# A two-layer diffusion backbone on one core: layer 0's output projection with tokens stationary, its boundary in token order, and gate products that do not wait for their branch

## The chip, the core and the metric

The kernel runs on one core of a Trainium2 chip. The metric is the device time of one execution in microseconds (us). The kernel before takes 1455.42 us, the median of three runs (1454.31 to 1457.41). The core's engines work side by side, each through a queue of its own in the order in which the program gives it instructions: PE (TensorE, matrix products; PEld is its loading of the stationary operand), DVE (VectorE), ACT (ScalarE), POOL (GpSimd), and SP (SyncE), which here issues all DMA transfers. Engines wait for each other through semaphores.

## The reference, cut to what matters

Two layers; each reads a latent stream x (256 tokens of width 2048) and a context stream ctx (256 tokens). In layer 0 both streams go through everything; in layer 1 ctx only supplies keys and values, and the result is x.

```python
def _branch_merge(o_mla, p, lp):
    g_m = jax.nn.silu(p[..., OFF_GM:OFF_HY])
    g_h = jax.nn.silu(p[..., OFF_GH:N_IN])
    y_h = _hyena(p[..., OFF_HY:OFF_GH], lp)
    y = jnp.concatenate([rmsnorm(o_mla, lp["grp_g_mla"]) * g_m,
                         rmsnorm(y_h, lp["grp_g_hy"]) * g_h], axis=-1)
    return rmsnorm(y @ lp["w_out"], lp["post_g"])

def _layer(x, ctx, c, c_ctx, lp, cos, sin, update_ctx):
    ...
    hx = rmsnorm(x, lp["pre_g"]) * (1.0 + sc_x) + sh_x
    px = hx @ lp["w_in"]
    ...
    o_x = o_x.swapaxes(0, 1).reshape(B, L, MLA_W)
    x_new = x + g_x * _branch_merge(o_x, px, lp)
```

`p` is one input projection. It holds queries and keys of an attention branch (A), three inputs of a long-convolution branch (B), and a gate for each branch. `shift`, `scale` and gate `g_x` come from a vector of the stream through `ada_w` (the modulation).

## The kernel before

**Layout.** Activations stand with features on the 128 partitions and tokens in the free dimension ("transposed"). A layer's 16 tiles of features (KT = 16) hold 512 columns: 256 of ctx (stream 0), then 256 of x (stream 1). Each product of two f32 operands is made as three: both operands are split in a high and a low part (`split`, line 428: a CAST on ACT for the high part, a subtraction on DVE for the low), and `mm3` (line 448) multiplies high by high, high by low, low by high. A matmul is named out<-moving,stationary. Products that are not split (sums over partitions with a ones matrix, tables of the Fourier transform) leave two records each in the trace.

**Items.** The big products go by weight items of 1024 columns (0.5 MB): `w_items` (line 840) cuts a projection into items; `loader` loads them, `prepper` splits them, `products` (line 988) runs their matmuls into `acc` tiles of PSUM, strictly in the order of a list of 362 items. After the last item of a group, an evacuation ("evac") brings the sums to SBUF. An item with a `need` is not begun before the named steps have been recorded. Items 90 to 125 are layer 0's branch inputs, 126 to 157 its gates, 158 to 221 its output projection (first x, then ctx), 222 on layer 1: queries, keys and values, branch inputs, 294 to 325 gates, 326 to 361 output projection.

**Order.** All other work (attention heads, convolution, norms, the boundary) stands in jobs, Python generators that yield one instruction at a time. `Net.run` (line 364) records the next instruction of that job which could start first by a table of costs, and of those within 0.05 us the one of best rank. Products have the worst rank (10): they fill what jobs leave. The recorded order is what the engines get; nothing is reordered on the chip. A pool of 78 tiles of 128x512 (`slots`, "s" in names) limits who may begin.

**Gates.** `layer_items` (line 1523) gives the last item of each gate group a need: `on{l}_{i}` (branch A's rows i are normalised) or `hn{l}_{i}` (branch B's). Its evac (`gate_evac`, line 1387) takes SiLU of the sums on ACT and multiplies the branch's row with it on DVE. The normalisation (`branch_norm`, line 1212) uses `rstd_bc` (line 484): a sum of squares over partitions by a ones matmul, a power of -1/2 on POOL, and two transposes that spread the result over partitions.

**Output projection and boundary of layer 0.** For each stream and each 256 output features, the weights are stationary and the stream's 256 tokens move: 128x256 matmuls. `z_evac` (line 1410) copies the sums and adds up their squares. Behind a stream's last item `boundary` (line 1421) starts: `rstd_bc` over the features; z times gate times norm, plus the old residual, which `hx_job` (line 825) had written to DRAM as `xt_d` and which is fetched back; a second `rstd_bc`; `modulate` (line 810) makes layer 1's input `hx1`. For stream 1 the new residual is transposed back to token rows and written to `xres_d`, which the end of layer 1 reads. x's boundary runs beside ctx's projection, ctx's boundary beside layer 1's first items. Layer 1's projection already runs with tokens stationary (`rows=True`).

Of the kernel before, what the change touches and what calls it, by code (L numbers as in the profile page):

```python
# [9 lines left out]
F32 = mybir.dt.float32  # L10
# [159 lines left out]
class Net:  # L170
# [330 lines left out]
    def setup(self):  # L501
# [10 lines left out]
        nc.vector.memset(self.ones, 1.0)  # L512
        self.mhalf = c.tile([P, 1], F32, name="mhalf")
# [269 lines left out]
    def first_norm(self):  # L783
# [24 lines left out]
        self.xt_d = self.scratch("xt_d", [KT, P, T])  # L808
# [16 lines left out]
    def hx_job(self, t0, t1):  # L825
        hx = self.st[0].setdefault("hx", {})

        def one(kt):
            hx[kt] = yield from self.new_split(T)
            yield from self.modulate(0, kt, self.xt[kt], self.bc0, hx[kt], ((0, slice(0, L)), (1, slice(L, T))))  # L830
        yield from self.each(one(kt) for kt in range(t0, t1))
        self.done.add(f"hx0_{t0}")
        if t1 == KT:
            self.slots.put(self.bc0)
            for kt in range(KT):
                yield self.dma(self.xt_d[kt], self.xt[kt])
                self.slots.put(self.xt[kt])
# [374 lines left out]
    def branch_norm(self, l, sq, src, base, gain, nq, flag):  # L1212
# [5 lines left out]
        for h0 in range(0, 8, 2):  # L1218
# [168 lines left out]
    def gate_evac(self, l, tile0, nq):  # L1387
        st = self.st[l]

        def evac(m, ps):  # L1390
            g = (yield from self.sget())[0]
            yield self.act(g[:, 0:nq], ps[:, 0:nq], AF.Silu)
            y = st["y"][tile0 + m][:, 0:nq]
            yield self.tt(y, y, g[:, 0:nq], ALU.mult)
            self.slots.put(g)
            if (tile0 + m) % 8 == 7:
                self.done.add(f"y{l}_{tile0 // 8}")
        return evac

# [9 lines left out]

    def z_evac(self, s, g):  # L1410
        st = self.st[0]

        def evac(m, ps):
            z = st.setdefault("z", {})
            if m == 0:
                z[s, g] = (yield from self.sget())[0]
            yield self.either(z[s, g][:, m * L:(m + 1) * L], ps[:, 0:L])
            yield from self.sumsq(st.setdefault("z_sq", {}).setdefault(s, [None]), ps[:, 0:L], L)
        return evac

    def boundary(self, s):
        st = self.st[0]
        bc = yield from self.rstd_bc([(st["z_sq"][s], L)], D)
        sq = [None]
        xn = {}
        xr = {}
        r = slice(s * L, (s + 1) * L)
        pc = self.par[0]["pcol"]

        def fetch(g):  # L1430
            if g < 8:
                xr[g] = (yield from self.sget())[0]
                for m in range(2):
                    yield self.dma(xr[g][:, m * L:(m + 1) * L], self.xt_d[2 * g + m][:, r])
        yield from fetch(0)
        yield from fetch(1)
        for g in range(8):
            z = st["z"][s, g]
            yield from self.on(xr[g], bc)
            for m in range(2):  # L1440
                h = z[:, m * L:(m + 1) * L]
                yield self.stt(h, h, pc[:, 2 * g + m, s:s + 1], bc[:, 0:L])
            yield self.tt(z, z, xr[g], ALU.add)
            self.slots.put(xr.pop(g))
            yield from fetch(g + 2)
            yield from self.sumsq(sq, z, T)
            xn[g] = z
        (h,) = yield from self.sget()
        yield self.tt(h[:, 0:L], sq[0][:, 0:L], sq[0][:, L:T], ALU.add)
        self.slots.put(bc, sq[0])  # L1450
        bc = yield from self.rstd_bc([([h], L)], D)
        hx = self.st[1].setdefault("hx", {})
        p = self.par[1]
        for kt in range(KT):
            src = xn[kt // 2][:, (kt % 2) * L:(kt % 2 + 1) * L]
            hx[s, kt] = yield from self.new_split(L)
            yield from self.modulate(1, kt, src, bc, hx[s, kt], ((s, slice(0, L)),))
            if kt % 4 == 3:
                self.done.add(f"hx1_{s}_{kt // 4}")
            if kt % 2:  # L1460
                if s == 0:
                    self.slots.put(xn[kt // 2])
        self.slots.put(bc)
        if s == 0:
            return
        self.xres_d = self.scratch("xres_d", [2, 4, P, 512])
        for g in range(4):
            for tt in range(2):
                (ps,) = yield from self.pget()
                for q in range(4):  # L1470
                    kt = 4 * g + q
                    yield self.tr(ps[:, q * P:(q + 1) * P],
                            xn[kt // 2][:, (kt % 2) * L + tt * P:(kt % 2) * L + (tt + 1) * P], self.ident)
                (t,) = yield from self.sget()
                yield self.act(t, ps)
                self.mis.put(ps)
                yield from self.on(t)
                yield self.dma(self.xres_d[tt, g], t)
                self.slots.put(t)
            self.slots.put(xn[2 * g], xn[2 * g + 1])  # L1480


    def out_evac(self, g):
        st = self.st[1]

        def evac(m, ps):
# [8 lines left out]
            yield self.tt(st["zo"][m][g], ps, self.gate[g], ALU.mult)  # L1495
        return evac

    def load_gate(self):
        self.gate = []
        p = self.par[1]["pcol"]  # L1500
        for j in range(4):
# [297 lines left out]
```

## Time and profile before

| | us |
|---|---|
| median of the runs | 1455.42 |
| profiled execution, its time | 1454.14 |
| profiled execution, first to last instruction (span) | 1452.4 |
| PE busy | 1410.2 |
| DVE busy | 1230.0 |
| ACT busy | 690.6 |
| POOL busy | 17.3 |

Busy time is the union of an engine's instructions; a matmul's record is longer than its share of PE, since matmuls are pipelined, and so a step on PE is read from full stretches, as length over count. In views of groups, a row gives engine, operation, out<-in, shape and count, then busy us, mean ns of one, and the idle time before with what ended it. In a timeline a row gives start, length, and in brackets the idle time before it.

### The profile page before, as it was taken

The page shows a single profiled execution, that of the slowest core. Times are in us where ns is not written, and L with a number is a line of the kernel's source. Part 1 is how long each engine was busy: PE and PEld are TensorE (multiplying, and loading weights), DVE is VectorE, ACT ScalarE, POOL GpSimd, SP SyncE. Part 2 cuts the span into 40 slices and gives each one's busy share as a digit, 9 for nine tenths or more (in the row PEclk, how much of TensorE's full clock was granted, in tenths as well). Part 3 has the DMA queues.
Part 4 walks back from the last instruction along what each step waited for, and adds up shares of the span by engine and source line. Part 5 has one row for each costly group of instructions (what it writes and reads, how often), then busy time and mean ns, then how long its engine had stood idle before and what let it go on. Part 6 is the DMA issues. An engine that isn't in the chain of part 4 may idle for free.

```text
span 1452.4 us, 24747 instructions
## 1 busy us (share of the span) xinstructions
PE 1410.2 (97%) x9184; PEld 1239.1 (85%) x9184; DVE 1230.0 (85%) x2283; ACT 690.6 (48%) x1325; POOL 17.3 (1%) x20
## 2 busy tenths in 40 slices
PE   7899899999999999999999999999999999899997
PEld 5676678788888888888889999998999998899886
DVE  4669899999999999998899979769989998885554
ACT  4421345455445452444325436564556666455542
POOL 0000000000000000000000000000000000000000
PEclk9999999999999999999999999999999999999999
DMA  9999864456555677446759854488859544676631
GB/s 315 335 333 358 292 245 142 163 177 236 192 192 178 206 254 259 147 146 219 266 211 369 283 204 138 168 301 311 304 189 345 199 151 164 214 241 223 236 122 58
DMA packets 146281, 329.87 MB, mean 227 GB/s; under 512 B 16325, under 2 KB 38892, under 8 KB 146160
## 3 DMA queue, kind: packets, MB, share of 16 engines
q1 hardware_dynamic: 146160, 328.29, 64.9%
q8 instruction: 72, 1.18, 0.3%
q14 instruction: 49, 0.40, 0.1%
HBM read 303.04 MB, written 25.18 MB: 226 GB/s over the span
## 4 chain that ended last, share of the span: by engine, by line
PE 78%; DMA 12%; DVE 6%; issue 2%; SPq 1%; ACT 1%; POOL 0%; DVEq 0%; POOLq 0%; ACTq 0%
PE acc L233 61%; PE mis L233 14%; DVE s L251 4%; PE mis L236 2%; DMA raw<-in_p_ada_first 2%; DMA s<-in_p_win 2%; DMA raw<-in_p_win 1%; DMA s<-in_p_ada_first 1%; SPq L310 1%; DMA ring<-in_p_ada_slow 1%; DMA s<-in_filt_w 1%; DMA s<-in_p_uk 1%; DVE junk L281 1%; DMA s<-in_ctx 1%; DVE raw L251 1%
## 5 line engine op out<-in xcount | busy, mean ns | idle before, releaser
L233 PE MATMUL acc<-s,hi 128*128 128x256 f32 (+1 forms) x2336 | 559.6, 330 | 6.8 <-DVE s L251 4.0
L233 PE MATMUL acc<-s,s 128*128 128x256 f32 (+1 forms) x2928 | 496.6, 324 | 0.4 <-ACT s L244 0.2
L233 PEld LDWEIGHTS acc<-s,s 128*128 128x128 f32 x2928 | 430.3, 191 | 45.4 <-issue 2.3
L233 PEld LDWEIGHTS acc<-s,hi 128*128 128x128 f32 x2336 | 393.0, 191 | 45.9 <-DVE s L251 5.3
L233 PE MATMUL acc<-s,raw 128*128 128x256 f32 (+1 forms) x1120 | 368.9, 329 | 1.6 <-DVE raw L251 1.6
L251 DVE TENSOR_TENSOR s<-s,s 128x512 fp32r<-128x512 f32 (+6 forms) x545 | 322.1, 619 | 26.7 <-ACT s L244 15.2
L281 DVE SCALAR_TENSOR_TENSOR junk<-ring,ring 128x1024 bf16<-128x1024 f32 x240 | 292.1, 1217 | 13.7 <-DMA ring<-in_p_ada_slow 11.2
L233 PE MATMUL mis<-s,s 128*128 128x256 f32 (+1 forms) x1232 | 239.0, 336 | 2.4 <-ACT s L244 1.0
L233 PEld LDWEIGHTS acc<-s,raw 128*128 128x128 f32 x1120 | 213.9, 191 | 20.6 <-DVE raw L251 2.6
L233 PEld LDWEIGHTS mis<-s,s 128*128 128x128 f32 x1232 | 190.5, 189 | 31.8 <-DVE s L251 4.2
L244 ACT CAST s<-s 128x512 fp32r<-128x512 f32 (+2 forms) x294 | 162.8, 586 | 88.9 <-DVE s L251 27.4
L244 ACT CAST hi<-raw 128x1024 fp32r<-128x1024 f32 (+1 forms) x97 | 94.1, 970 | 139.6 <-PE acc L233 97.4
L251 DVE TENSOR_TENSOR raw<-raw,hi 128x1024 fp32r<-128x1024 f32 x85 | 103.6, 1220 | 36.2 <-ACT hi L244 35.9
L244 ACT CAST hi<-s 128x512 fp32r<-128x512 f32 x134 | 79.3, 618 | 108.7 <-PE acc L233 90.5
L251 DVE TENSOR_TENSOR raw<-s,hi 128x512 fp32r<-128x512 f32 x134 | 90.4, 684 | 40.9 <-ACT hi L244 35.4
L244 ACT COPY s<-mis 128x512 f32<-128x512 f32 (+3 forms) x99 | 47.4, 481 | 127.8 <-PE mis L233 88.8
L244 ACT CAST s<-mis 128x512 fp32r<-128x512 f32 (+1 forms) x100 | 56.5, 569 | 78.2 <-PE mis L236 45.8
L251 DVE TENSOR_TENSOR s<-raw,s 128x512 fp32r<-128x512 f32 x132 | 87.2, 683 | 3.4 <-ACT s L244 3.4
L251 DVE TENSOR_TENSOR s<-mis,s 128x512 fp32r<-128x512 f32 (+2 forms) x128 | 84.6, 666 | 5.9 <-ACT s L244 2.7
L244 ACT CAST s<-raw 128x512 fp32r<-128x512 f32 x132 | 77.7, 618 | 15.4 <-DMA raw<-in_p_win 12.8
L236 PE MATMUL mis<-ident,s 128*128 128x128 f32 x365 | 67.6, 292 | 5.8 <-ACT s L244 2.7
L236 PEld LDWEIGHTS mis<-ident,s 128*128 128x128 f32 x365 | 49.1, 155 | 19.7 <-ACT s L244 3.8
(85 smaller groups left out, 824.2 us busy)
## 6 DMA issues: line engine op xcount, KB each, us to landing
ring<-in_p_ada_slow SPq DMA_DIRECT2D x136, 512.0 KB, 4.1
raw<-in_p_win SPq DMA_DIRECT2D x105, 512.0 KB, 5.1
s<-in_p_win SPq DMA_DIRECT2D x166, 256.0 KB, 5.5
s<-in_p_wout SPq DMA_DIRECT2D x100, 256.0 KB, 5.7
raw<-in_p_wout SPq DMA_DIRECT2D x46, 512.0 KB, 3.6
s<-in_p_ada_first SPq DMA_DIRECT2D x62, 256.0 KB, 5.9
raw<-in_p_ada_first SPq DMA_DIRECT2D x25, 512.0 KB, 6.6
ring<-crow_d SPq DMA_DIRECT2D x14, 512.0 KB, 5.9
```

The source lines that it names most:

```text
L233: lambda: self.nc.tensor.matmul(out, lhsT, rhs, start=start, stop=stop), 0.3)
L236: return Op("pe", 0.11, [out], [in_], lambda: self.nc.tensor.transpose(out, in_, ident), 0.3)
L244: self.nc.scalar.copy(out, in_)
L251: return Op("dve", fixed + n * rate, [out], ins, lambda: getattr(self.nc.vector, name)(out=out, **kw))
L281: lambda: self.nc.vector.scalar_tensor_tensor(out=junk, in0=a, scalar=1.0, in1=b, op0=ALU.mult, op1=ALU.mult, accum_out=acc))
L310: return Op("sp", n / 360e3, [dst], [src], lambda: self.nc.sync.dma_start(dst, src))
```

## The change

Layer 0's output projection takes the split activations as stationary operand, 128 tokens at a time, and moves 512 weight columns (`rows=True`, weights laid out as layer 1's). Its result stands in token rows. `z_evac` takes the squares with ACT's accumulation and multiplies with the modulation gate, which `gate_rows` writes to DRAM as a row and `gate_load` reads back broadcast over partitions. `boundary` works on token rows: x and ctx are read again from the inputs (`residual`), both norms are numbers per partition (`rstd_rows`, no PE work), the residual is written as it stands, and the normalised rows are transposed by PE, four 128x128 at a time, into layer 1's layout. `xt_d` is gone, and a tile of x becomes free as soon as it is modulated. `load_gate` of layer 1 uses the same broadcast. Gate items have no need any more; the product of gate and branch is recorded by whichever comes last (`gated`). An item of the projection needs two tiles of activations where it needed four.

```diff
@@ hx_job
             yield from self.modulate(0, kt, self.xt[kt], self.bc0, hx[kt], ((0, slice(0, L)), (1, slice(L, T))))
+            self.slots.put(self.xt[kt])
...
-            for kt in range(KT):
-                yield self.dma(self.xt_d[kt], self.xt[kt])
-                self.slots.put(self.xt[kt])
@@ branch_norm
                 self.done.add(f"{flag}{l}_{h}")
+                yield from self.gated(l, base + h, nq)
@@ gate_evac
             yield self.act(g[:, 0:nq], ps[:, 0:nq], AF.Silu)
-            y = st["y"][tile0 + m][:, 0:nq]
-            yield self.tt(y, y, g[:, 0:nq], ALU.mult)
...
+            st.setdefault("g", {})[tile0 + m] = g
+            yield from self.gated(l, tile0 + m, nq)
...
+    def gated(self, l, i, nq):
+        st = self.st[l]
+        flag = ("on", "hn")[i // 8]
+        if i not in st.get("g", {}) or f"{flag}{l}_{i % 8}" not in self.done:
+            return
+        g = st["g"].pop(i)
+        y = st["y"][i][:, 0:nq]
+        yield self.tt(y, y, g[:, 0:nq], ALU.mult)
...
+    def gate_load(self, l, s):
+        g = yield from self.sget(4)
+        for j in range(4):
+            yield self.dma(g[j], self.gate_d[l, s][:, j * 512:(j + 1) * 512].to_broadcast([P, 512]))
+        self.gate[l, s] = g
@@ z_evac
-            yield self.either(z[s, g][:, m * L:(m + 1) * L], ps[:, 0:L])
-            yield from self.sumsq(st.setdefault("z_sq", {}).setdefault(s, [None]), ps[:, 0:L], L)
+            yield from self.until((f"gate0_{s}",))
+            (junk,) = yield from self.sget()
+            yield self.act(junk, ps, AF.Square, accum_out=self.zss[:, s, m, g:g + 1])
+            self.slots.put(junk)
+            (z[s, m, g],) = yield from self.sget()
+            yield self.tt(z[s, m, g], ps, self.gate[0, s][g], ALU.mult)
...
+    def residual(self, s, m, h):
+        z = self.st[0]["z"]
+        xr = yield from self.sget(4)
+        src = self.a["x" if s else "ctx"]
+        for g in range(4):
+            yield self.dma(xr[g], src[0, m * P:(m + 1) * P, g * 512:(g + 1) * 512])
+        rs = yield from self.rstd_rows(self.zss[:, s, m])
+        for g in range(4):
+            x = z[s, m, g]
+            yield from self.on(xr[g])
+            yield self.stt(x, x, rs, xr[g], ALU.mult, ALU.add)
+            yield self.act(xr[g], x, AF.Square, accum_out=self.xss[:, s, m, g:g + 1])
+        self.slots.put(*xr)
+        rs = yield from self.rstd_rows(self.xss[:, s, m])
+        for g in range(4):
+            x = z[s, m, g]
+            (h[m, g],) = yield from self.sget()
+            yield self.act(h[m, g], x, AF.Copy, scale=rs)
+            if s == 1:
+                yield self.dma(self.xres_d[m, g], x)
@@ boundary
-        bc = yield from self.rstd_bc([(st["z_sq"][s], L)], D)
...
+        yield from self.each(self.residual(s, m, h) for m in range(2))
...
+        for kp in range(KT // 2):
+            (ps,) = yield from self.pget()
+            for i in range(2):
+                kt = 2 * kp + i
+                for m in range(2):
+                    yield self.tr(ps[:, i * L + m * P:i * L + (m + 1) * P],
+                                  h[m, kt // 4][:, (kt % 4) * P:(kt % 4 + 1) * P], self.ident)
...
+                yield self.act(t[:, r], ps[:, r], AF.Identity, bias=p["mcol"][:, 0, kt, s:s + 1],
+                               scale=p["acol"][:, kt, s:s + 1])
+            self.mis.put(ps)
+            v = yield from self.to_split(t, T)
@@ load_gate
-        for j in range(4):
-            self.gate.append((yield from self.spread(p[:, 4 * j:4 * j + 4, 1], T)))
+        yield from self.gate_rows(1)
+        yield from self.gate_load(1, 1)
@@ layer_items
-                it = win(g0 + g, self.gate_evac(l, 8 * half + 2 * g, nq))
-                it[-1].need = (f"{flag}{l}_{2 * g + 1}",)
-                gates.append(it)
+                gates.append(win(g0 + g, self.gate_evac(l, 8 * half + 2 * g, nq)))
@@ build
-            for g in range(8):
+            for g in range(4):
...
-                items += self.w_items(a["p_wout0"][g], 256, lambda kt, r=r: self.st[0]["ys"][kt][:, r],
-                                      self.z_evac(s, g), need)
+                items += self.w_items(a["p_wout0"][g], 512, lambda kt, r=r: self.st[0]["ys"][kt][:, r],
+                                      self.z_evac(s, g), need, rows=True)
```

The change moves instructions on every engine, since the recorded order is a result of the whole. Three places on PE matter here. First, the beginning of layer 0's output projection (item 158), before:

```order
L233 MATMUL acc_99_7540<-s_897_7151,hi_62_7390 128x256
L233 MATMUL acc_99_7540<-s_898_7152,hi_62_7390 128x256
L233 MATMUL acc_99_7540<-s_897_7151,raw_154_7391 128x256
L233 MATMUL acc_100_7541<-s_897_7151,hi_62_7390 128x256
L233 MATMUL acc_100_7541<-s_898_7152,hi_62_7390 128x256
L233 MATMUL acc_100_7541<-s_897_7151,raw_154_7391 128x256
```

and of the change (here the weights' parts stand in slots s, 928 and 930; the activations' parts are 906 and 907):

```order
L233 MATMUL acc_99_7541<-s_928_7431,s_906_7320 128x512
L233 MATMUL acc_99_7541<-s_930_7433,s_906_7320 128x512
L233 MATMUL acc_99_7541<-s_928_7431,s_907_7321 128x512
L233 MATMUL acc_100_7542<-s_928_7431,s_906_7320 128x512
L233 MATMUL acc_100_7542<-s_930_7433,s_906_7320 128x512
L233 MATMUL acc_100_7542<-s_928_7431,s_907_7321 128x512
```

Six matmuls of 256 columns for one tile of inputs and 256 output features have become six of 512 columns for one tile of inputs and 512 output features. Second, PE around the norm of branch A in layer 1 (`on1`: the ones matmul and the two transposes <-ident,rs), before; mis_326 is the last head's output, and acc rows are gate products, the first of item 297:

```order
L233 MATMUL mis_326_14350<-s_1777_14323,s_1709_13880 128x256
L233 MATMUL mis_326_14350<-s_1778_14324,s_1709_13880 128x256
L233 MATMUL mis_326_14350<-s_1777_14323,s_1710_13881 128x256
L233 MATMUL mis_327_14377<-ones,s_1560_12837 128x1 x2
L236 MATMUL mis_328_14391<-ident,rs 128x128 x2
L233 MATMUL acc_165_13974<-s_1200_9881,hi_141_13803 128x256 x2
L233 MATMUL acc_165_13974<-s_1200_9881,raw_297_13804 128x256
```

and of the change, the rows up to the same two transposes; 324, 325, 327 and 328 are matmuls of the convolution job, acc_149 is a product of item 296:

```order
L233 MATMUL mis_325_13428<-s_1772_13356,s_1467_11283 128x512
L233 MATMUL mis_325_13428<-s_1773_13357,s_1467_11283 128x512
L233 MATMUL mis_325_13428<-s_1772_13356,s_1468_11284 128x512
L233 MATMUL mis_326_13434<-ones,s_1546_11873 128x1 x2
L233 MATMUL acc_149_13200<-s_1168_8915,hi_138_13065 128x256
L233 MATMUL mis_327_13451<-s_1784_13413,s_1467_11283 128x512
L233 MATMUL mis_327_13451<-s_1785_13414,s_1467_11283 128x512
L233 MATMUL mis_327_13451<-s_1784_13413,s_1468_11284 128x512
L233 MATMUL mis_328_13452<-s_1784_13413,s_1467_11283 128x512
L233 MATMUL mis_328_13452<-s_1785_13414,s_1467_11283 128x512
L233 MATMUL mis_328_13452<-s_1784_13413,s_1468_11284 128x512
L236 MATMUL mis_329_13459<-ident,rs 128x128 x2
```

Before, nothing stands between the last head, the ones matmul and the transposes. Now nineteen instructions stand between the last head's last matmul and the ones matmul (four transposes, nine products, six matmuls of 128x512), and seven behind it. Third, PE at the boundary of the context stream, in layer 1's first items; before, a piece of the first norm (ones) beside transposes of x's residual:

```order
L233 MATMUL acc_132_10130<-s_1162_9547,hi_97_10020 128x256 x2
L233 MATMUL acc_132_10130<-s_1162_9547,raw_225_10021 128x256
L233 MATMUL mis_234_10169<-ones,s_1119_8985 128x1
L236 MATMUL mis_235_10186<-ident,s_1085_8670 128x128 x2
L236 MATMUL mis_235_10186<-ident,s_1106_8827 128x128 x2
L233 MATMUL mis_234_10169<-ones,s_1119_8985 128x1
```

and of the change, the first transposes of normalised context rows (s_1239 and s_1251) inside item 230:

```order
L233 MATMUL acc_120_9628<-s_1145_8765,hi_103_9557 128x256
L233 MATMUL acc_120_9628<-s_1144_8764,raw_228_9558 128x256
L236 MATMUL mis_232_9664<-ident,s_1239_9525 128x128
L236 MATMUL mis_232_9664<-ident,s_1251_9604 128x128
L236 MATMUL mis_232_9664<-ident,s_1239_9525 128x128
L236 MATMUL mis_232_9664<-ident,s_1251_9604 128x128
```

PE's part in the boundary moves from the sums at its two norms to groups of four transposes, the first in the ninth item after the stream's last projection item.

More of the change, by code (lines that the diff above doesn't have):

```diff
@@ L512, in setup @@
         nc.vector.memset(self.ones, 1.0)
+        self.zss = c.tile([P, 2, 2, 4], F32, name="zss")
+        self.xss = c.tile([P, 2, 2, 4], F32, name="xss")
+        self.gate = {}
         self.mhalf = c.tile([P, 1], F32, name="mhalf")
@@ new lines, in evac, with rstd_rows @@
+            yield from self.until((f"gate0_{s}",))
[4 more added lines that the diff above has]
+            yield self.tt(z[s, m, g], ps, self.gate[0, s][g], ALU.mult)
+        return evac
+    def rstd_rows(self, sums):
+        ms = self.small.tile([P, 4], F32, tag="mf", name="mf")
+        rs = self.small.tile([P, 4], F32, tag="rf", name="rf")
+        yield self.vsum(ms[:, 0:1], sums)
+        yield from self.rstd_cols(rs[:, 0:1], ms[:, 0:1], D)
+        return rs[:, 0:1]
@@ L1452, in boundary @@
+    def boundary(self, s):
+        if s == 1:
+            self.xres_d = self.scratch("xres_d", [2, 4, P, 512])
+        self.slots.put(*self.gate[0, s])
+        h = {}
+        yield from self.each(self.residual(s, m, h) for m in range(2))
         hx = self.st[1].setdefault("hx", {})
         p = self.par[1]
[L1454 to L1480, printed above, removed]
+        for kp in range(KT // 2):
+            (ps,) = yield from self.pget()
+            for i in range(2):
[3 more added lines that the diff above has]
+                                  h[m, kt // 4][:, (kt % 4) * P:(kt % 4 + 1) * P], self.ident)
+            if kp % 2:
+                self.slots.put(h[0, kp // 2], h[1, kp // 2])
+            (t,) = yield from self.sget()
+            for i in range(2):
+                kt = 2 * kp + i
+                r = slice(i * L, (i + 1) * L)
+                yield self.act(t[:, r], ps[:, r], AF.Identity, bias=p["mcol"][:, 0, kt, s:s + 1],
+                               scale=p["acol"][:, kt, s:s + 1])
+            self.mis.put(ps)
+            v = yield from self.to_split(t, T)
+            self.slots.put(t)
+            for i in range(2):
+                c = v[:, i * L:(i + 1) * L]
+                hx[s, 2 * kp + i] = Split(c.hi, c.lo, [v.tiles[i]])
+            if kp % 2:
+                self.done.add(f"hx1_{s}_{kp // 2}")
@@ L1508, in load_gate @@
             self.xres.append(r)
-        yield from self.on(*self.gate)
+        yield from self.on(*self.gate[1, 1])
     def finish(self, m):
@@ L1549, in layer_items @@
         gates = []
-        for half, (g0, flag) in enumerate(((G_GM, "on"), (G_GH, "hn"))):
+        for half, g0 in enumerate((G_GM, G_GH)):
             for g in range(4):
-                it = win(g0 + g, self.gate_evac(l, 8 * half + 2 * g, nq))
-                it[-1].need = (f"{flag}{l}_{2 * g + 1}",)
-                gates.append(it)
+                gates.append(win(g0 + g, self.gate_evac(l, 8 * half + 2 * g, nq)))
         return q, kvs, mids, gates
@@ L1770, in lay_out @@
     o["p_wkr"] = w[:, :, OFF_KR:OFF_GM].reshape(2, 4, 4, P, 64).transpose(0, 1, 3, 2, 4).reshape(2, 4, P, 256)
-    o["p_wout0"] = tiles(i["w_out"][0:1])[0]
-    o["p_wout1"] = i["w_out"][1].reshape(8, 2, P, 4, 512).transpose(3, 0, 2, 1, 4).reshape(4, 8, P, 1024)
+    for l in range(2):
+        o[f"p_wout{l}"] = i["w_out"][l].reshape(8, 2, P, 4, 512).transpose(3, 0, 2, 1, 4).reshape(4, 8, P, 1024)
     uq = i["w_uq"].reshape(2, 4, P, HEADS, HEAD_Q)
```

66 lines of the change are left out of this document (26 added, 40 removed).

## The prediction

> **What bounds the kernel now.** I read the page first: span, busy shares, the clock strip and the chain of waits.
>
> ```profile
> span 1452.4 us, 24747 instructions
> PE 1410.2 (97%) x9184; PEld 1239.1 (85%) x9184; DVE 1230.0 (85%) x2283; ACT 690.6 (48%) x1325; POOL 17.3 (1%) x20
> PE 78%; DMA 12%; DVE 6%; issue 2%; SPq 1%; ACT 1%; POOL 0%; DVEq 0%; POOLq 0%; ACTq 0%
> ```
>
> The reader should see that TensorE is busy for 97% of the span and carries 78% of the chain that ended last. DVE at 85% is near, so DVE must be followed too. A mean hides stages, so next come the stretches of the span (columns: window, length, busy us and instructions of PE, weight loads, DVE, ACT, POOL; granted clock; DMA share; GB/s).
>
> ```profile
> 0.00:100.00 100.00, 86.64 (x771) 63.16 (x771) 57.24 (x123) 39.12 (x90) 1.32 (x6) 0.98 0.93 322
> ...
> 100.00:160.00 60.00, 53.86 (x552) 40.34 (x552) 52.35 (x103) 16.63 (x34) 0.00 (x0) 1.00 0.97 358
> 400.00:500.00 100.00, 100.00 (x510) 84.31 (x509) 95.16 (x182) 48.41 (x90) 0.00 (x0) 1.00 0.58 197
> 600.00:700.00 100.00, 99.90 (x462) 81.91 (x461) 89.50 (x156) 41.16 (x66) 1.47 (x1) 1.00 0.66 220
> 700.00:800.00 100.00, 100.00 (x568) 88.29 (x567) 94.58 (x155) 39.44 (x73) 0.00 (x0) 1.00 0.75 272
> 800.00:900.00 100.00, 100.00 (x837) 100.00 (x836) 87.31 (x159) 48.63 (x98) 0.70 (x1) 1.00 0.60 204
> 900.00:1000.00 100.00, 97.48 (x799) 96.57 (x797) 76.69 (x141) 54.86 (x106) 3.76 (x3) 0.98 0.70 240
> 1200.00:1300.00 100.00, 93.78 (x683) 88.19 (x683) 82.72 (x167) 57.47 (x118) 2.15 (x2) 0.98 0.61 202
> ```
>
> Up to about 160 us DMA is 93 to 97% busy and PE waits; from then on PE is full, except near 985 us (layer boundary) and 1260 us (layer 1's gates), which are also the stretches with a clock under 1.00. So the time is PE's own work plus a few waits, and I cost the change in these two currencies.
>
> **Part 1: the projection.** Layer 0's projection (768 to 957 us) has 64 weight items of 24 matmuls of 128x256, 1536 in all. The change makes 64 items of 12 matmuls of 128x512, 768. Layer 1's projection already has the new form (tokens stationary, 512 weight columns moving), so both prices stand in one answer, PE alone: first the old form, then the new.
>
> ```profile
> 770.00:860.00 90.00, 90.00 (x753) 1.00 0.89 319
> 1357.00:1440.00 83.00, 83.00 (x368) 1.00 0.38 128
> ```
>
> PE is full in both, so time over count is the step: 90.00/753 = 0.1195 us and 83.00/368 = 0.2255 us. Old: 1536 x 0.1195 = 183.6 us. New: 768 x 0.2255 = 173.2 us. **Term: -10.4 us.** Nothing lies beside it, since PE was full there; weight bytes, splitting of weights and item order stay the same. The new rate asks 0.5 MB per 12 x 0.2255 = 2.7 us, 194 GB/s, and the old stage ran at 319 GB/s with PE full.
>
> The Trainium skill, "TensorE: Matmul & The Clock Gate", section "Back-to-back issue gap", gives an isolated warm gap of N/2.4 + 2.5 ns, 109 and 216 ns for these two widths. By it halving the count saves only 768 x 2.5 ns = 1.9 us, an estimate from that page. The two rows disagree: 2 x 0.1195 - 0.2255 = 0.0135 us per pair, and the measurement decides.
>
> **Part 2: PE's small work.** Four blocks of "sum of squares over partitions, then spread to a row" leave the boundary: 16 records of the ones matmul and 8 transposes. Also gone are the 32 transposes that turn the residual back to rows and the 16 that spread layer 1's gate. Added are 64 transposes that turn the normalised rows to columns, and 3 for the gates.
>
> ```profile
> 1263.02 0.58 PE L233 MATMUL mis<-ones,s 128*128 128x1 f32 x4 [2.57 <-DVE s L251]
> 957.63 0.60 PE L236 MATMUL mis<-ident,s 128*128 128x128 f32 x4
> L236 PE MATMUL mis<-ident,s 128*128 128x128 f32 x357 | 65.8, 292 | 5.4 <-ACT s L244 2.4 <-DMA s<-in_x 1.1 <-DMA s<-in_ctx 0.8
> L233 PE MATMUL mis<-ones,s 128*128 128x1 f32 x68 | 8.7, 238 | 4.4 <-DVE s L251 4.4
> ```
>
> In a row of four, the last ends 0.29 us (0.24 for ones) after its start, so a step is (0.60 - 0.29)/3 = 0.10 us and (0.58 - 0.24)/3 = 0.11 us. Net: 16 x 0.11 out, 67 - 56 = 11 x 0.10 in. **Term: -0.7 us.**
>
> **Part 3: the gates' wait.** Before, a gate product whose evacuation needs the branch's normalised rows may not start until those are recorded, and every PE job behind it stands still. Layer 1's branch A, on PE:
>
> ```profile
> 1259.59 0.86 PE L233 MATMUL mis<-s,s 128*128 128x256 f32 x5 [0.47 <-DVE s L251]
> 1265.36 0.69 PE L236 MATMUL mis<-ident,rs 128*128 128x128 f32 x2 [1.76 <-POOL rs L303]
> 1264.80:1268.20 3.40, 2.84 (x14) 0.51 0.90 280
> 1268.20:1272.00 3.80, 3.80 (x33) 0.99 0.90 299
> ```
>
> PE idles 0.47, 2.57 (the ones row quoted above) and 1.76 us, and then runs at a clock of 0.51 for 3.40 us: 14 starts where 3.40/0.1195 = 28 would fit. In the new order, between head 7's last matmul and the ones matmul stand 4 transposes, 9 matmuls of 256 and 6 of 512: 4 x 0.10 + 9 x 0.1195 + 6 x 0.2255 = 2.8 us, over the 2.57. Between ones and spread stand one of 256 and six of 512, 1.5 us of the 1.76. The 0.47 stays. Term: -2.57 - 1.5 = **-4.1 us**, and without the idle the slow clock window should go: 14 steps lost x 0.1195 = 1.7, of which some 0.2 us is the rest of the wait: **-1.5 us**. In layer 0 (gates from 564 to 768 us) PE is full, as 600:700 and 700:800 show, so nothing is gained there.
>
> What is late next: the gate products that were held back no longer cover branch B. In the new order its sum stands at item 308 of 362, and the output projection, which needs it, begins at 326: 18 items x 24 x 0.1195 = 52 us. Before it was 305, so the cover shrinks by 9 us and remains.
>
> **Part 4: the boundary.** Its waits before, on PE:
>
> ```profile
> 908.72 0.43 PE L236 MATMUL mis<-ident,rs 128*128 128x128 f32 x2 [0.58 <-POOL rs L303]
> 960.18 0.38 PE L233 MATMUL mis<-ones,s 128*128 128x1 f32 x2 [0.28 <-DVE s L251]
> 986.65 0.58 PE L233 MATMUL mis<-ones,s 128*128 128x1 f32 x4 [1.51 <-DVE s L251]
> 988.40:991.80 3.40, 3.40 (x19) 0.50 0.58 191
> ```
>
> The first two belong to the boundary and go; the third is layer 1's query norm, followed by a half-clock window that starts 19 matmuls where 28 fit, 1.1 us. The new boundary puts its first transposes nine items after the stream's last product, and these wait for loads of x, two row norms and the scaling. Prices, by form:
>
> ```profile
> L281 DVE SCALAR_TENSOR_TENSOR junk<-ring,ring 128x1024 bf16<-128x1024 f32 x240 | 292.1, 1217 | 13.7 <-DMA ring<-in_p_ada_slow 11.2 <-DMA s<-in_p_win 1.1
> L251 DVE TENSOR_TENSOR s<-s,s 128x512 fp32r<-128x512 f32 x216 | 141.3, 683 | 9.7 <-ACT s L244 9.6
> L251 DVE TENSOR_TENSOR raw<-raw,hi 128x1024 fp32r<-128x1024 f32 x85 | 103.6, 1220 | 36.2 <-ACT hi L244 35.9
> L251 DVE SCALAR_TENSOR_TENSOR s<-s,rf,s 128x512 f32<-128x512 f32 x8 | 5.5, 748 | 1.3 <-POOL rf L303 1.3
> L244 ACT CAST s<-raw 128x512 fp32r<-128x512 f32 x132 | 77.7, 618 | 15.4 <-DMA raw<-in_p_win 12.8 <-DMA raw<-in_p_wout 2.5
> L246 ACT ACTIVATION_READ_ACCUMULATOR s<-acc 128x1 f32 x8 | 1.5, 193 | 0.0
> ```
>
> For the latent stream the cover is the second stream's projection: the order has 25 us of ACT and 21 us of DVE work beside 31 us of PE before the first transposes. No wait. For the context stream, from its last product to its last transposes, PE has 426 rows: 390 x 0.1195 and 36 small ones, 50.5 us. DVE has 81, among them 27 subtractions of 512 at 0.683, 11 dots at 1.217, 8 residual steps at 0.748 and 4 subtractions of 1024 at 1.22, with the small ones 54 us. ACT has 80, about 47 us (618 ns a cast, 0.19 more for each accumulated square). So DVE is over PE by some 4 us here. Bounds: from -3.5 us (all the waits above and the slow window go, none comes) to +5 us (DVE's 4 us and a second slow window against the 0.9 us of the first two waits). I take 0: DVE's excess pays back the 0.9, the 1.5 and the 1.1 us.
>
> The transfers (KB each, median us from issue to landing):
>
> ```profile
> xt_d<-s SPq DMA_DIRECT2D x16, 256.0 KB, 3.7
> ...
> s<-xt_d SPq DMA_DIRECT2D x32, 128.0 KB, 5.4
> ...
> s<-in_x SPq DMA_DIRECT2D x8, 256.0 KB, 6.3
> ```
>
> The 16 spills go; 16 loads of 256 KB of x and ctx, 6.3 us each, replace the 32 loads of 128 KB. The gates' 12 broadcast loads of 256 KB stand in SP's queue over ten items ahead of their first reader, so products hide them too.
>
> **Part 5: the start.** Slots come free tile by tile, so loads are issued in another order. Up to the last first-layer modulation weight, SP issues 49.8 MB where it issued 50.9. At 358 GB/s (window 100:160) that is 2.9 us at most, either way if the new order is the worse. PE's waits there have many causes; I take 0.
>
> **Sum.** -10.4 - 0.7 - 4.1 - 1.5 = -16.7 us on the profiled execution's 1454.14 gives 1437.4. The median of the runs, 1455.42, lies 1.3 us above that execution: **1438.7 us**.
>
> **Rivals.**
> - **The waits come back elsewhere.** PE's order changes throughout; parts 3 and 4 rest on an order recorded before the chip's delays. If the 5.6 us of part 3 return, at the boundary or among the heads of layer 1, 1444; with the boundary at +5 as well, 1449. For it: DVE at 95% in 400:500. Against: PE is at 100.00 in that very stretch. Chance 0.28.
> - **It does better:** the boundary's -3.5 and the start's -2.9: 1432. Chance 0.12.
> - **It doesn't do what it says: the projection's step gains nothing.** If a 512-wide matmul with layer 0's operands took as long as two of 256, 0.239 us, part 1 would be 0: 1449. The two PE rows speak against it. Chance 0.03. The Trainium skill's gap formula of part 1 lies near this rival, 1.9 us under it.
> - **Slower: the boundary's transposes hold PE.** They stand in PE's queue between products, so each group of four that finds its rows unready stops all of layer 1 behind it. There are 16 groups, one per 3 to 3.5 us of PE. Slower than before needs 16.7 us of waiting, over 1.0 us for each of the 16; at 1.5 us each the time is 1438.7 + 24 = 1463. For it: DVE's 54 us against 50.5 in the second stream. Against: that is 4 us in all, and the first stream has 10 us to spare. Chance 0.05.
>
> - **The transposes slow the clock.** If each of the 16 groups cost a window like that at 988.40, 1.1 us, the time is 1438.7 + 17.6 = 1456, no change. Chance 0.02, because the old residual transposes speak against it:
>
> ```profile
> 945.00:962.00 17.00, 16.72 (x144) 1.00 0.79 273
> ...
> 945.00:962.00 17.00, 4.83 (x32) 1.00 0.79 273
> ```
>
> The first row is all of PE, the second its transposes (line 236) alone: 32 of the 144, in groups of four among products, and the clock stayed at 1.00. This rival is a rule of the Trainium skill, "TensorE: Matmul & The Clock Gate", section "Part 4: PE-mode transpose": a transpose does not count as PE-busy in the way a matmul does, and the fast clock does not engage for it.
>
> **How the numbers follow.** The forecast has 0.50. A change of 0.2%, 2.9 us, is about what a measurement of this kernel can tell from none. Faster by more than that: 0.50 + 0.12 + 0.03 + nearly all of 0.28, 0.92; within it 0.03, the slow clock and the worst of the returned waits; slower 0.05. The range, 1431 to 1449, takes in the better case and the returned waits and leaves out the slow rival.
>
> **What would show it.** In the profile after: 768 projection matmuls of 128x512 in some 175 us with PE full; no idle before layer 1's first ones and spread beyond 1 us, and no half-clock window there; the transposes of the second boundary with waits of about 4 us in total. The forecast is wrong if the projection's step is not near 0.2255 us, if PE idles over 5 us at the boundary, or if the first 200 us move by more than 3.

## The result, and the profile after

The changed kernel takes 1434.47 us (median of four runs, 1434.05 to 1436.47) against 1455.07 us before (1454.31 to 1457.41, four runs): a ratio of 0.9855, 95% interval 0.9836 to 0.9874, or 20.6 us. The forecast was 1438.7 us in a range of 1431 to 1449. The profiled execution took 1436.47 us, 17.7 us less than that of before; the sum had said 16.7. The other 2.9 us lie between the profiled executions and the medians: before, the profiled one was 0.9 us under the median, after, 2.0 us over it (it is the longest of the four).

The page after, same lines as before:

```profile
span 1434.7 us, 23168 instructions
PE 1400.1 (98%) x8411; PEld 1200.3 (84%) x8411; DVE 1196.2 (83%) x2186; ACT 691.6 (48%) x1329; POOL 18.1 (1%) x24
PE 82%; DMA 7%; DVE 6%; issue 2%; ACT 1%; SPq 1%; DVEq 0%; POOLq 0%; POOL 0%; ACTq 0%
```

PE has 773 instructions and 10 us of busy time less and a larger share of the chain. So the bound is the same engine with less work. The stretches (window, length, then busy us and count for PE, weight loads, DVE, ACT, POOL; clock; DMA share; GB/s):

```profile
900.00:1000.00 100.00, 99.43 (x655) 91.10 (x654) 87.73 (x151) 70.28 (x144) 4.41 (x5) 1.00 0.93 344
...
1100.00:1200.00 100.00, 96.41 (x688) 89.80 (x687) 80.59 (x163) 58.58 (x117) 0.00 (x0) 0.98 0.39 130
1200.00:1300.00 100.00, 100.00 (x780) 96.90 (x780) 86.17 (x176) 59.45 (x124) 1.77 (x2) 1.00 0.60 199
```

The reader is to see that PE's two holes of before (900 to 1000 and 1200 to 1300) are closed but for 0.6 us, and that a new one has opened at 1100 to 1200, with the clock at 0.98. Before, that stretch was full:

```profile
1100.00:1200.00 100.00, 100.00 (x752) 95.80 (x751) 96.45 (x194) 63.05 (x125) 0.00 (x0) 1.00 0.60 210
```

PE alone in the changed kernel, inside layer 0's projection and inside layer 1's:

```profile
780.00:860.00 80.00, 80.00 (x355) 1.00 0.84 300
...
1340.00:1420.00 80.00, 80.00 (x354) 1.00 0.37 125
```

80.00/355 = 0.2254 us a matmul of 512 columns, the same in both layers. Following items through the recorded order, the first matmul of layer 1 (item 222) comes 178.8 us after the first of the projection (item 158), where it came 189.0 us after it: -10.2 us. The projection itself begins at 768.2 us in both profiled executions, so between these two nothing was gained or lost ahead of it. At layer 1's branch A norm, in the timeline of PE:

```profile
1247.16 0.50 PE L233 MATMUL mis<-ones,s 128*128 128x1 f32 x4
...
1249.11 0.38 PE L236 MATMUL mis<-ident,rs 128*128 128x128 f32 x2
```

No bracket stands behind these rows (one would from 0.15 us on): PE did not idle before them, where it had idled 2.57 and 1.76 us. The new hole, on PE and then on ACT:

```profile
1115.98 0.28 PE L233 MATMUL acc<-s,raw 128*128 128x256 f32 x1
1117.24 0.50 PE L233 MATMUL acc<-s,hi 128*128 128x256 f32 x2 [0.98 <-ACT hi L244]
1118.60 0.48 PE L233 MATMUL acc<-s,raw 128*128 128x256 f32 x1 [0.86 <-DVE raw L251]
```

```profile
1113.23 1.28 ACT L246 ACT_TABLE_LOAD   x1 [7.95 <-DVE sm L251]
1114.52 0.69 ACT L246 ACTIVATE s<-mis,sm 128x512 f32<-128x512 f32 x1
...
1116.16 1.03 ACT L244 CAST hi<-raw 128x1024 fp32r<-128x1024 f32 x1
```

ACT stood 7.95 us at an exponential of the first attention head, which waited for its maximum from DVE. The CAST that splits the next weight item stood behind it in ACT's queue, and PE waited for that CAST. Two waits of under 1 us were followed by one window of 3.4 us at half clock. A second profile of the same kernel (after_b, below) has the same two waits without the window; first this execution, then that one, PE alone:

```profile
1118.70:1122.10 3.40, 3.40 (x17) 0.51 0.01 2
```

```profile
1119.50:1122.90 3.40, 3.40 (x29) 1.00 0.01 2
```

### The profile page after: what moved, and what is told of

Its sections match the earlier page's. It is cut to its first block, busy times and chain, and to the rows that moved or that the text cites. A ratio compares the mean times of both kernels' runs of the same rounds, so it can differ in the third digit from the quotient of the medians.

```text
span 1434.7 us, 23168 instructions
## 1 busy us (share of the span) xinstructions
PE 1400.1 (98%) x8411; PEld 1200.3 (84%) x8411; DVE 1196.2 (83%) x2186; ACT 691.6 (48%) x1329; POOL 18.1 (1%) x24
## 4 chain that ended last, share of the span: by engine, by line
PE 82%; DMA 7%; DVE 6%; issue 2%; ACT 1%; SPq 1%; DVEq 0%; POOLq 0%; POOL 0%; ACTq 0%
PE acc L233 64%; PE mis L233 15%; DVE s L251 4%; PE mis L236 3%; DMA s<-in_p_uv 2%; DVE junk L281 1%; DMA raw<-in_p_ada_first 1%; SPq L310 1%; DVE raw L251 1%; DMA s<-in_ctx 1%; DMA s<-in_p_win 1%; DMA s<-in_filt_w 1%; ACT s L246 1%; DMA ring<-in_p_ada_slow 1%; DMA s<-in_p_ada_first 1%
## 5 line engine op out<-in xcount | busy, mean ns | idle before, releaser
L233 PE MATMUL acc<-s,hi 128*128 128x512 f32 (+1 forms) x1824 | 479.1, 350 | 5.4 <-DVE s L251 3.8
L233 PE MATMUL acc<-s,s 128*128 128x512 f32 (+1 forms) x2556 | 476.0, 340 | 0.2 <-ACT s L244 0.2
L233 PEld LDWEIGHTS acc<-s,hi 128*128 128x128 f32 x1824 | 318.4, 192 | 49.3 <-DVE s L251 4.6
L233 PE MATMUL acc<-s,raw 128*128 128x512 f32 (+1 forms) x864 | 303.4, 351 | 2.9 <-DVE raw L251 2.9
L244 ACT CAST s<-s 128x512 fp32r<-128x512 f32 (+3 forms) x338 | 187.0, 590 | 61.9 <-DVE s L251 25.1
L233 PEld LDWEIGHTS acc<-s,raw 128*128 128x128 f32 x864 | 165.5, 192 | 24.1 <-DVE raw L251 3.6
L233 PE MATMUL acc<-hi,s 128*128 128x512 f32 x344 | 111.6, 390 | 0.0
L244 ACT CAST s<-mis 128x512 fp32r<-128x512 f32 x100 | 55.9, 569 | 62.4 <-PE mis L236 32.5
L236 PE MATMUL mis<-ident,s 128*128 128x128 f32 (+1 forms) x397 | 71.1, 290 | 4.6 <-DVE s L268 1.5
L233 PEld LDWEIGHTS acc<-hi,s 128*128 128x128 f32 x344 | 64.5, 188 | 13.2
```

The lines of the kernel that those rows point to most:

```text
L233: lambda: self.nc.tensor.matmul(out, lhsT, rhs, start=start, stop=stop), 0.3)
L236: return Op("pe", 0.11, [out], [in_], lambda: self.nc.tensor.transpose(out, in_, ident), 0.3)
L244: self.nc.scalar.copy(out, in_)
```

## The experiments

Each run has the kernel before on the same chip beside it, so I compare ratios to it; 0.1% is 1.5 us. "Changed" is the changed kernel.

### The step of a matmul

halves cuts the projection's matmuls in two, with the same tile standing still:

```diff
@@ w_items
-                        if rows:
+                        if rows and cols:
+                            t = x[:, m * P:(m + 1) * P]
+                            for n3, (u, v) in enumerate(((t.hi, w.hi), (t.hi, w.lo), (t.lo, w.hi))):
+                                step = wid if (first and n3 == 0) or (last and n3 == 2) else cols
+                                for c in range(0, wid, step):
+                                    yield self.mm(ps[:, c:c + step], u, v[:, j * wid + c:j * wid + c + step],
+                                                  first and n3 == 0, last and n3 == 2)
+                        elif rows:
...
@@ build
-                                      self.z_evac(s, g), need, rows=True)
+                                      self.z_evac(s, g), need, rows=True, cols=256)
```

> The changed kernel with layer 0's projection matmuls cut in two of 256 columns, same stationary tile, all but the first and the last of each sum (32 of 512, 1472 of 256 in place of 768 of 512). Theory (a step of 0.1195 us for 256 and 0.2255 for 512 whatever stands still): +736 x 0.0135 = +9.9 us, 1444.4. Rival (the gain came from which operand stands still, or a second matmul on the same stationary tile is cheaper): less than half of it, under 1439.5.

Measured: 1443.77 us, ratio 0.9915 [0.9903, 0.9928], against 0.9855 for the changed kernel: 0.6% or 8.7 us more. From item 158 to item 222 it took 188.3 us, 9.5 us more than the changed kernel, and within 0.7 us of the old 189.0. So the gain comes from the number of matmuls, not from which operand stands still.

### The gates with and without their need

need_both restores the needs in the changed kernel; its edit stands below. gates_only puts the gates' part of the change (`gated`, no needs) alone into the kernel before.

```diff
@@ layer_items
-        for half, g0 in enumerate((G_GM, G_GH)):
+        for half, (g0, flag) in enumerate(((G_GM, "on"), (G_GH, "hn"))):
             for g in range(4):
-                gates.append(win(g0 + g, self.gate_evac(l, 8 * half + 2 * g, nq)))
+                it = win(g0 + g, self.gate_evac(l, 8 * half + 2 * g, nq))
+                it[-1].need = (f"{flag}{l}_{2 * g + 1}",)
+                gates.append(it)
```

> The changed kernel with the gate items' needs put back in both layers (projection, boundary and spill stay changed). Theory of the prediction (part 3: the waits around layer 1's branch A norm went because gate products no longer wait): they come back, +5.6 us on the changed kernel's 1434.5, so 1440, with idle of about 2.6 and 1.8 us before the ones matmul and the spread near item 296 and a half-clock window behind. Rival (those waits went because the whole order moved: in this kernel's order nine matmuls of 128x512 still stand between the last head and the ones matmul, and three behind it): at most 1 to 2 us of wait, no slow window, 1435 to 1437.

> The kernel before with the gates' part of the change alone. Theory of the prediction: -5.6 us on 1455.1, so 1449.5, no idle at the norm of branch A in layer 1, where its order now has products between the ones matmul and the spread. Rival (the gates' part is worth nothing by itself, what it removes comes back as other waits): 1455.

gates_only: 1451.59 us, ratio 0.9960 [0.9947, 0.9974], by the ratio 5.8 us less than before (3.8 to 7.7), where 5.6 was expected. Its recorded order is that of before up to item 297. In its timeline the two rows at the norm have no idle ahead of them, but behind them a transpose of the convolution waits 2.26 us, where before had no wait:

```profile
1265.97 0.50 PE L233 MATMUL mis<-ones,s 128*128 128x1 f32 x4
...
1268.32 0.38 PE L236 MATMUL mis<-ident,rs 128*128 128x128 f32 x2
...
1289.15 0.55 PE L236 MATMUL mis<-ident,s 128*128 128x128 f32 x3 [2.26 <-DVE s L268]
```

From item 288 to item 326 the same PE work took 177.1 us, against 181.3 before: 4.2 us less. So part of the gain came back as another wait, as the rival had it, and the 5.8 agrees with 5.6 only within its interval.

need_both: 1446.88 us, ratio 0.9942 [0.9928, 0.9955]. That is 0.9% or 13 us over the changed kernel, more than either side expected, and not where part 3 had looked. Layer 1's waits did not come back in size; around its norm PE waited 0.23 us:

```profile
1258.66 0.50 PE L233 MATMUL mis<-ones,s 128*128 128x1 f32 x4
1259.02 0.94 PE L233 MATMUL mis<-s,s 128*128 128x512 f32 x3
1260.19 0.43 PE L236 MATMUL mis<-ident,rs 128*128 128x128 f32 x2 [0.23 <-POOL rs L303]
```

The loss stands in layer 0, at branch B's norm: from item 142 to item 158 PE took 109.0 us, where the changed kernel took 92.7; from item 158 to item 361 it was 2.9 us faster. First the timeline (acc rows are products, mis<-s,s and mis<-ident,s the convolution), then the window in which the clock is 0.50:

```profile
688.65 0.39 PE L233 MATMUL acc<-s,raw 128*128 128x512 f32 x1
688.88 0.84 PE L233 MATMUL mis<-s,s 128*128 128x512 f32 x3
...
695.24 0.98 PE L236 MATMUL mis<-ident,s 128*128 128x128 f32 x7 [0.62 <-ACT s L244]
696.05 0.50 PE L233 MATMUL mis<-ones,s 128*128 128x1 f32 x4
703.84 1.01 PE L233 MATMUL mis<-ones,s 128*128 128x1 f32 x4 [7.28 <-DVE s L251]
707.11 1.11 PE L236 MATMUL mis<-ident,rs 128*128 128x128 f32 x4 [2.26 <-POOL rs L303]
707.88 6.46 PE L233 MATMUL acc<-s,s 128*128 128x512 f32 x17
```

```profile
699.20:712.80 13.60, 6.70 (x20) 0.50 0.88 296
```

PE idles 7.28 and 2.26 us, and four windows pass at half clock. In this order items 143 and 144 are recorded whole; then come the convolution's last 20 instructions on PE and the norm's 8 with no product between them, since item 145, the next, needs the norm's rows. In the kernel before the norm was recorded at items 142 to 143 and PE did not wait. What DVE did in the wait:

```profile
698.67 1.22 DVE L281 SCALAR_TENSOR_TENSOR junk<-ring,ring 128x1024 bf16<-128x1024 f32 x1
...
699.81 0.42 DVE L251 TENSOR_TENSOR s<-s,s 128x256 f32<-128x256 f32 x1
...
700.75 1.21 DVE L281 SCALAR_TENSOR_TENSOR junk<-ring,ring 128x1024 bf16<-128x1024 f32 x1
...
702.23 1.22 DVE L281 SCALAR_TENSOR_TENSOR junk<-ring,ring 128x1024 bf16<-128x1024 f32 x1
```

The last sums of squares stand in DVE's queue between modulation dots of 1.22 us. With the products held at item 145, nothing on PE could cover them.

### When the input tiles come free

Heads, convolution and norms of layer 0 stand about four items later in the changed order than before (branch A's norm at item 126, before at 122). The suspect was the tiles of x, freed one by one. spill keeps them to the end and writes them as before; late keeps them without the writes; late_need is late with the needs restored; early_before is the kernel before with each tile written and freed at once.

```diff
@@ hx_job, late (spill has the write of early_before ahead of the put)
-            self.slots.put(self.xt[kt])
         yield from self.each(one(kt) for kt in range(t0, t1))
...
+            for kt in range(KT):
+                self.slots.put(self.xt[kt])
...
@@ hx_job, early_before
             yield from self.modulate(0, kt, self.xt[kt], self.bc0, hx[kt], ((0, slice(0, L)), (1, slice(L, T))))
+            yield self.dma(self.xt_d[kt], self.xt[kt])
+            self.slots.put(self.xt[kt])
...
-            for kt in range(KT):
-                yield self.dma(self.xt_d[kt], self.xt[kt])
-                self.slots.put(self.xt[kt])
```

> The changed kernel with the 16 transposed input tiles kept until the last modulation and written to DRAM as before (nobody reads them). Theory of the prediction (part 5 taken at 0): within 1.5 us of 1434.5. Rival (the earlier free slots and the missing writes are where the 4 us beyond the prediction come from): 1437 to 1439, with the products of the first 200 us later by as much.

> The changed kernel with the 16 tiles of x freed together after the last modulation, as before, but without the writes. Theory (what moves the time is the recorded order: tiles freed one by one let loads and products run four items ahead of the heads in layer 0, tiles freed late keep them together): as the run with the writes, 0.983 of the kernel before or 1431 to 1433 us, no waits around item 277. Rival (the run with the writes was fast by the chance of its order, and earlier free tiles are a gain): 1434.5 or more.

> The same with the gate items' needs put back in both layers. Theory (what a need costs hangs on where branch B's norm falls among the items; here it is recorded at items 143 to 144, near the place it had before, 142 to 143): 2 to 6 us over the run without needs. Rival (in the changed kernel the needs cost 12 us whatever the order): +12.

> The kernel before, where each tile of x is written to DRAM and freed as soon as it is modulated instead of all 16 at the end; needs, projection and boundary as before. Theory (freeing early lets products run ahead, branch B's norm falls to item 144, where the next gate item needs it, and PE stands still there as in the run with both needs): idle of about 10 us near item 144 with three or four half-clock windows behind, 8 to 14 us slower than the kernel before. Rival (early tiles help the DMA-bound start, or do nothing): equal or up to 4 us faster.

| run | us | ratio, interval | branch A's and B's norm at items |
|---|---|---|---|
| before | 1455.07 | 1 | 122, 142 to 143 |
| changed | 1434.47 | 0.9855 [0.9836, 0.9874] | 126, 147 to 148 |
| need_both | 1446.88 | 0.9942 [0.9928, 0.9955] | 126, behind 144 |
| spill | 1431.61 | 0.9832 [0.9813, 0.9851] | 122, 142 to 143 |
| late | 1436.23 | 0.9857 [0.9843, 0.9870] | 122, 143 to 144 |
| late_need | 1436.57 | 0.9867 [0.9852, 0.9882] | 122, 143 to 144 |
| early_before | 1450.04 | 0.9954 [0.9942, 0.9967] | 124, 144 |

Late freeing does bring the norms back to the old items. With it the needs cost 0.1%, 1.5 us, and the intervals overlap, so they cost nothing that can be told (the orders of late and late_need are the same up to item 297, so layer 0's needs change nothing there); without it they cost 13 us. In late_need layer 1's norm waits 0.23 us although its needs stand:

```profile
1247.05 0.50 PE L233 MATMUL mis<-ones,s 128*128 128x1 f32 x4
1248.58 0.43 PE L236 MATMUL mis<-ident,rs 128*128 128x128 f32 x2 [0.23 <-POOL rs L303]
```

spill came out faster than either side expected, 1431.61 us where the theory had 1433 to 1436. late was not faster than the changed kernel, though the theory expected it to be as fast as spill; the rival was right there. early_before was a plain miss. It was expected 8 to 14 us slower and was 6.7 us faster: at branch B's norm PE idled only 1.62 us, without a slow window, and at layer 1's norm 0.23 us ahead of the convolution's matmuls between.

```profile
695.60 0.50 PE L233 MATMUL mis<-ones,s 128*128 128x1 f32 x4
695.96 0.72 PE L233 MATMUL acc<-s,hi 128*128 128x512 f32 x2
696.51 0.52 PE L233 MATMUL mis<-ones,s 128*128 128x1 f32 x4
...
697.67 0.40 PE L233 MATMUL acc<-s,raw 128*128 128x512 f32 x1
699.69 0.65 PE L236 MATMUL mis<-ident,rs 128*128 128x128 f32 x4 [1.62 <-POOL rs L303]
...
1258.29 0.50 PE L233 MATMUL mis<-ones,s 128*128 128x1 f32 x4
1259.37 1.99 PE L233 MATMUL mis<-s,s 128*128 128x512 f32 x7 [0.23 <-DVE s L251]
1261.20 0.38 PE L236 MATMUL mis<-ident,rs 128*128 128x128 f32 x2
```

So a norm near item 144 with a need at 145 does not decide by itself: the waits at the norm are 9.5 us in need_both and 1.6 in early_before. The recorded orders say what differs. In early_before the convolution ends within item 143, 20 products stand between its last matmul and the norm's first sum, and six more ahead of the spread; in need_both no product stands there. DVE's queue hardly differs: from the convolution's last matmul to the spread it has four modulation dots in early_before and five in need_both.

### How much slack the boundary has

```diff
             yield self.act(xr[g], x, AF.Square, accum_out=self.xss[:, s, m, g:g + 1])
+            for _ in range(2):
+                op = self.act(xr[g], x, AF.Square)
+                op.cost = 0.0
+                yield op
```

> The changed kernel with two more squares on ACT (results unused) behind each residual step of the boundary, at no cost in the planner's table: 16 per stream, 0.63 us each, 10 us more ACT work per stream than the recorded order knows of. Theory (x's boundary has some 10 us to spare, ctx's has none, and transposes in PE's queue hold it): waits of 3 to 10 us before the transposes of ctx's boundary, 1438 to 1446 us. Rival (both boundaries have slack, as the changed kernel showed under 1 us of waits there): under 1436.

Measured: 1440.26 us, ratio 0.9886 [0.9870, 0.9902], 0.3% or 4.5 us over the changed kernel. PE's waits from 768 to 1060 us, first of the changed kernel, then of slack (who waited for whom, us in total, times, longest):

```profile
PE acc L233 <- DVE ms L251: 0.6, 1, 0.6
PE acc L233 <- DVE hi L251: 0.6, 1, 0.6
```

```profile
PE acc L233 <- DVE raw L251: 2.4, 4, 1.4
PE acc L233 <- ACT s L246: 2.2, 1, 2.2
PE mis L233 <- DVE s L251: 1.3, 1, 1.3
PE acc L233 <- DVE hi L251: 0.4, 1, 0.4
PE acc L233 <- ACT hi L244: 0.2, 1, 0.2
```

None of these is a transpose. The waits are for the split of weight items (raw, hi), the evacuation of the query products and the query norm, whose work on ACT shares the queue with the extra squares. So the place was not the expected one: what the boundary disturbs is its neighbours on ACT and DVE, before its own transposes. That the price lies in the expected range is partly luck. From item 158 to item 238 slack took 229.4 us, 8.6 more than the changed kernel. But its recorded order differs from item 196 on, and the hole at 1116 us is not in it: from item 277 to item 304 it took 154.4 us, some 4 less than the changed kernel.

### A version that is faster?

spill looked 3 us faster than the changed kernel, so both ran again on one chip.

> The changed kernel itself, on one chip with the next one, so that the two can be compared. Both theories: 0.9855 of the kernel before, within its interval (0.984 to 0.987).

> The changed kernel with tiles kept late and written (the run spill) once more, beside the changed kernel on the same chip. Theory (its order lacks the waits of the changed kernel at items 277 to 287, 8 us in the trace, of which 5 are given back elsewhere): 3 us faster than the changed kernel. Rival (the first figure was the chance of one chip, as the run without the writes was no faster than the changed kernel): within 1.5 us of it.

The changed kernel took 1434.69 us, 0.9849 [0.9836, 0.9862]; spill 1431.74 us, 0.9832 [0.9812, 0.9852], with runs from 1428.93 to 1436.34. The medians differ by 3 us twice, as the theory said, and the intervals overlap, so it stays likely and unproven. PE in the stretch of the changed kernel's new hole, first the changed kernel's two profiled executions, then spill's two:

```profile
1080.00:1200.00 120.00, 116.41 (x839) 0.99 0.44 148
1080.00:1200.00 120.00, 116.76 (x852) 1.00 0.46 151
```

```profile
1080.00:1200.00 120.00, 119.47 (x894) 1.00 0.44 145
1080.00:1200.00 120.00, 119.52 (x898) 1.00 0.47 159
```

spill lacks the hole in both. From the first matmul of item 158 to the first of item 361 the changed kernel took 656.1 and 654.6 us, spill 649.5 and 650.1, so behind the start spill is 4.5 us or more faster. What blurs the totals is the start: item 158 begins at 768.2 us in both executions of the changed kernel, and at 767.2 and 772.8 us in those of spill.

## Why the prediction was right, and where it was not

**Part 1, the projection: right.** -10.4 us predicted, -10.2 measured from item 158 to 222, and halves gives 9.5 back where 9.9 was expected. By the isolated gap that the Trainium skill, "TensorE: Matmul & The Clock Gate", section "Back-to-back issue gap", states (N/2.4 + 2.5 ns), halves would cost about 1.8 us, an estimate from that page; the measurement is five times that.

**Part 2, PE's small work:** -0.7 us, too small to be seen apart.

**Part 3, the gates: right in size for the kernel before, wrong as a reason for the change.** -5.6 us predicted; alone on the kernel before the gates bring -5.8; the norm's waits go there, and one of 2.26 us comes in their place. And two steps failed. "In layer 0 (gates from 564 to 768 us) PE is full, ... so nothing is gained there" was read from the order before. The other edits move that order; in it the old needs would stop PE for 9.5 us and cost 13. And layer 1's waits, for which part 3 booked -4.1 and -1.5, go without this edit too: need_both, late_need and early_before have all needs and at most small waits there. With the need put back in layer 1 alone, the changed kernel's recorded order is the same, instruction for instruction. What covers the norm in layer 1 is convolution matmuls of 128x512 in need_both, late_need and early_before, and products in gates_only; every order tried but the old one puts something there. PE's time over its steps (matmuls times the step of each form) between items 288 and 304 is some 11 us before, 1 in the changed kernel, and 3 to 5 in these four. And late_need, with all needs in place, already has 19.4 us of the 21.1 that the whole change brings by the ratios. So the waits were a property of one recorded order; which edit removed them has no single answer.

**Part 4, the boundary: better than taken.** I took 0 and gave -3.5 as the better end. All the old waits and the slow window at 988 us went, and PE waited 0.6 us twice. Of the old ones, the 1.5 us at the query norm and the window behind it were partly chance: gates_only has the same order there, waited 0.65 us and has no window. The step that failed is the count: DVE's 54 us against PE's 50.5 was work recorded ahead of the last transposes, but a transpose waits only for its scaled rows, and the last of these were done on ACT at 972.2 us, when the first transposes ran, 26 us ahead of the last ones. Between item 222 and the last transpose, PE needed 51.6 us (947.0 to 998.6) and lost about 1. (For x the first transposes stand in the twelfth item behind the stream's last product, not in the ninth as part 4 has it; the cover of 31 us was counted to the right place.) The rival by which the transposes slow the clock fell: over both sets of transposes, PE alone, the clock was full.

```profile
860.00:950.00 90.00, 89.39 (x422) 1.00 0.79 279
...
950.00:1000.00 50.00, 49.43 (x416) 1.00 0.97 353
```

In these stretches stand 64 transposes, among products. The rule of the Trainium skill, "TensorE: Matmul & The Clock Gate", section "Part 4: PE-mode transpose", that PE does not reach its full clock on transposes, does not show in such a mixture, where the clock was 1.00.

**Part 5, the start: right, as far as can be told.** 0 taken; the projection begins at 768.2 us before, and in both profiles of the changed kernel. But spill's two profiles differ by 5.6 us there, so the 2.9 us that part 5 allowed could not have been told from chance.

**What was missed** is the hole at 1116 us and the smaller waits behind it up to item 287: 7.9 us of PE's time over its steps, where before had less than 1; in after_b, without the half-clock window, 5.7. It falls under the rival "the waits come back elsewhere". So that the forecast came within 4.2 us of the median is partly luck, since misses cancel: the boundary 3.5 us better, layer 1's heads 5 to 7 worse, layer 1's later waits (items 288 to 303) some 10 us better where 5.6 was booked.

## What to carry to other kernels

On a kernel that is full on PE, count matmuls and take the step from a full stretch of the same form: that term held to a few per cent. A wait in a recorded order is a property of the whole order; before booking its removal, look in the new order whether other edits remove it anyway, and before calling a wait absent, look whether the new order would create it. What a need costs depends on how many products the order still has beside the work that it waits for: at branch B's norm none in need_both (13 us), 26 in early_before (a wait of 1.62 us). Then expect a few microseconds to open somewhere else.

## What the runs showed of the hardware

A matmul of 512 columns costs 0.0129 us less than two of 256 with the activations standing still (halves: 9.5 us over 736 matmuls more); the prediction's two rows gave 0.0135 with the weights standing still for the 256.

The granted clock falls to half in stretches of 3.4 us or a few times that. One such stretch came behind waits of 0.98 and 0.86 us at 1117 us, and none behind the same two waits when the same kernel ran again (after_b); 13.6 us came around waits of 7.28 and 2.26 us, none behind 1.62 us at 699 us of early_before. In the start it came at different places in the two kernels (clock 0.58 from 15.0 to 18.4 us before; 0.50 from 115.2 to 118.6 and from 159.6 to 166.4 us after, and in after_b also near 70 us) with no change of the time to the projection. So in the short cases the wait's length alone does not decide, and what does was not tried.
